# A 96-byte constant ahead of the left-hand SBUF pools of a hybrid decoder layer

## The chip, the cores and the metric

The kernel runs on one core of a Trainium2 chip. The metric is the device time of one launch in microseconds (us), as the median of several launches. The profile is one execution recorded by the hardware profiler; its engines are PE (TensorE matmul), PEld (TensorE weight load), DVE (VectorE), ACT (ScalarE), POOL (GpSimd) and SP (which issues the DMAs). SBUF is the on-chip memory from which PE reads both operands of a matmul: the weights (the stationary operand, 128x128 here, loaded ahead of the matmul) and the moving operand (up to 128x512 here). PSUM takes the products.

## The reference

One decoder layer on x of 1024 tokens by 1024 channels, in float32:

```python
h = rms_norm(x, norm1_g)
q, k, v, glu_a, glu_b = split(h @ w_in)            # 512 columns each
attn = stick_breaking_attention(rms_norm(q), rms_norm(k), v)   # 8 heads of 64, strictly causal
c = silu(layer_norm(causal_depthwise_conv(glu_a * sigmoid(glu_b))))   # width 31
x = x + concat([attn, c]) @ w_out
h = rms_norm(x, norm2_g)
gate, val = split(h @ w_up)                        # 2816 columns each
x = x + (silu(causal_depthwise_conv(gate)) * val) @ w_down    # width 3
```

## The kernel before, in words

Every large product is made in split precision: a float32 operand is split into a high part and a rest, both of type float32r, and three matmuls (high x high, high x rest, rest x high) are summed in one PSUM bank. The helper for it is `mm3`; the second argument of a matmul is the weights, the third is what moves past them.

```python
258     def mm3(ps, a_hi, a_lo, b_hi, b_lo, first, last):
259         nc.tensor.matmul(ps, a_hi, b_hi, start=first, stop=False)
260         nc.tensor.matmul(ps, a_hi, b_lo, start=False, stop=False)
261         nc.tensor.matmul(ps, a_lo, b_hi, start=False, stop=last)
```

In the profile a matmul is named `out<-moving,weights`, so `u<-b11h,a` has `b11h` moving past weights from `a`.

The layer runs in four stages. First come the input norm, the value, key and query projections and the GLU products with their convolution on DVE, ACT and POOL. Then comes the attention, whose instructions (with the last projections, the convolution's layer norm and its half of the output projection) are put in order by a planner in the kernel (`Plan`). The third stage finishes the output projection and the second norm and makes the up projection (`up`), 22 rounds over blocks of 128 hidden channels; it works in Strassen's manner, with seven products instead of eight, each of four `mm3`, so 84 matmuls of 128x512 in a round and 1848 in all. The fourth stage is the down projection (line 1203), 924 matmuls of 128x512 in the same manner.

SBUF is given out in pools. Pools without a side are stacked up from the low end ("left"), pools with `side="right"` are stacked down from the high end. The first left pool is `cst`, and each constant takes its place there in the order in which it is asked for. All other left pools (`small`, `mixp`, `qkvp`, `convp`, `op`, `wa`, `fp`) lie above it. In the built program each large tile of the left pools begins 128 bytes past a multiple of 256 in its partition, and each tile of the right pools that PE reads begins 224 bytes past one. The tiles that matter below are these:

```python
175     cst = ctx.enter_context(tc.tile_pool(name="cst", bufs=1))
281     hp = hp_ctx.enter_context(tc.tile_pool(name="hp", bufs=1, side="right", reuse_waits="tile"))
...
907     ffn = ffn_ctx.enter_context(tc.tile_pool(name="ffn", bufs=1, side="right", reuse_waits="tile"))
910         B[name] = [ffn.tile([P, 4, HS], F32R, tag=f"{name}{part}", name=f"b{name}{part}") for part in ("h", "l")]
...
996             pool, tag, bufs = {"11": (op, "v", 2) if f else (fp, "w", 8), "22": (op, "m", 1)}.get(name, (fp, "w", 8))
...
1052                 mm3(ps, ah[:, k, :], al[:, k, :], bh[:, k, :], bl[:, k, :], k == 0, k == 3)
...
1105         pool, bufs = (fp, 8) if n_slot % (8 + N_DN) < 8 else (dn, N_DN)
...
1203                         nc.tensor.matmul(ps, a[:, tok], b, start=first and m == 0, stop=last and m == 2,
```

- In the GLU products (`glu_b`, `glu_a`) the moving operand is the normed input (`h_hi`, `h_lo`, pool `hp`) and the weights come from pool `wp`: both are on the right.
- In the up projection (`u`, and `u_S` where a sum of blocks is used) the moving operand is `B` (pool `ffn`, right) and the weights are `A` (pools `fp` and `op`, left).
- In the down projection (`dn`) both operands of a matmul are named `wd`. They come from a ring of 28 slots: 8 in `fp` (left), then 20 in `dn` (right). Both operands of one matmul are on the same side; where the ring passes from one pool to the other, a matmul on one side alternates with the loading of weights on the other.

Operands for PE are made by ACT (the high part, L255 and L1114) and by DVE or POOL (the rest, L256 and L1115), and DVE (L1060 to L1067, L1206) brings the products out of PSUM.

Of the kernel before, what the change touches and what calls it, by code (L numbers as in the profile page):

```python
# [8 lines left out]
F32 = mybir.dt.float32  # L9
# [7 lines left out]
P = 128  # L17
# [120 lines left out]
def kernel(  # L138
# [60 lines left out]

    def const(shape, dt, name):  # L200
        return cst.tile(shape, dt, tag=name, name=name)

    ident = const([P, P], F32, "ident")
    make_identity(nc, ident)
    ident_b = const([P, P], BF16, "ident_b")
    nc.vector.tensor_copy(ident_b, ident)
    ident_r = const([P, P], F32R, "ident_r")
    nc.vector.tensor_copy(ident_r, ident)
    zero_b = const([P, P], BF16, "zero_b")
# [1033 lines left out]
```

## Time and profile before

| | |
|---|---|
| time, median of 3 runs | 1199.02 us (1198.83 to 1201.87) |
| the profiled execution's own time | 1199.73 us |
| its span, first to last instruction | 1197.9 us |
| mean granted TensorE clock | 0.985 |
| PE busy | 1146.3 us, 96% of the span |
| DVE, ACT, POOL busy | 954.4, 623.2, 611.1 us |

The span is 1.8 us shorter than the profiled execution's time, and that time is 0.7 us above the median of the runs. A matmul's duration in the profile is about 0.4 us, but matmuls overlap each other in the pipeline; what counts for the time is how far apart they start, and the view of the timeline shows their starts to a hundredth of a microsecond.

### The profile page before, as it was taken

The page shows a single profiled execution, that of the slowest core. Times are in us where ns is not written, and L with a number is a line of the kernel's source. Part 1 is how long each engine was busy: PE and PEld are TensorE (multiplying, and loading weights), DVE is VectorE, ACT ScalarE, POOL GpSimd, SP SyncE. Part 2 cuts the span into 40 slices and gives each one's busy share as a digit, 9 for nine tenths or more (in the row PEclk, how much of TensorE's full clock was granted, in tenths as well). Part 3 has the DMA queues.
Part 4 walks back from the last instruction along what each step waited for, and adds up shares of the span by engine and source line. Part 5 has one row for each costly group of instructions (what it writes and reads, how often), then busy time and mean ns, then how long its engine had stood idle before and what let it go on. Part 6 is the DMA issues. An engine that isn't in the chain of part 4 may idle for free.

```text
span 1197.9 us, 16127 instructions
## 1 busy us (share of the span) xinstructions
PE 1146.3 (96%) x5766; PEld 943.5 (79%) x5766; DVE 954.4 (80%) x1209; ACT 623.2 (52%) x1217; POOL 611.1 (51%) x490
## 2 busy tenths in 40 slices
PE   7999999999889798998999999999999999999998
PEld 6788999877668686776888888888888877888887
DVE  6699998777997987587977877787777578887877
ACT  6346674666666765364443333333333356666862
POOL 4347973555566753277523332233223157778873
PEclk9999999999999999998999999999999999999999
DMA  8122122111413222441322222222223261333033
GB/s 308 33 68 84 58 78 73 27 54 27 167 45 115 96 99 89 175 141 53 123 76 83 77 82 88 71 88 71 88 71 106 78 244 50 139 141 138 24 124 138
DMA packets 101853, 116.50 MB, mean 97 GB/s; under 512 B 20654, under 2 KB 80270, under 8 KB 101774
## 3 DMA queue, kind: packets, MB, share of 16 engines
q1 hardware_dynamic: 101486, 114.43, 28.6%
q8 instruction: 46, 0.75, 0.3%
q10 hardware_dynamic: 288, 1.05, 0.3%
q14 instruction: 33, 0.27, 0.1%
HBM read 82.95 MB, written 28.31 MB: 93 GB/s over the span
## 4 chain that ended last, share of the span: by engine, by line
PE 82%; DVE 7%; ACT 4%; POOL 3%; issue 2%; DMA 1%; SPq 0%; ACTq 0%; DVEq 0%; POOLq 0%
PE dn L1203 17%; PE u_S L261 7%; PE u_S L260 7%; PE u_S L259 7%; PE u L261 5%; PE u L260 5%; PE u L259 5%; PE wT L677 2%; DVE nb L651 2%; POOL conv_out L381 1%; PE v L261 1%; PE glu_b L259 1%; PE v L260 1%; PE v L259 1%; PE glu_b L260 1%
## 5 line engine op out<-in xcount | busy, mean ns | idle before, releaser
L1203 PE MATMUL dn<-wd,wd 128*128 128x512 f32 x924 | 216.0, 395 | 4.0 <-DVE c L1206 2.2
L1203 PEld LDWEIGHTS dn<-wd,wd 128*128 128x128 f32 x924 | 174.8, 190 | 45.1 <-DVE c L1206 3.7
L1206 DVE TENSOR_TENSOR c<-dn,c 128x512 f32<-128x512 f32 x144 | 95.3, 682 | 29.4 <-PE dn L1203 27.2
L375 DVE SCALAR_TENSOR_TENSOR conv<-cpad,cols_b,conv 128x1024 f32<-128x1024 f32 (+1 forms) x105 | 112.8, 1074 | 4.3 <-issue 1.5
L654 POOL TENSOR_TENSOR wt<-wt,nb 128x128 f32<-128x128 f32 (+3 forms) x64 | 77.4, 1212 | 75.6 <-DVE nb L651 51.9
L381 POOL TENSOR_TENSOR conv_out<-conv_out,attn_out 128x1024 f32<-128x1024 f32 (+1 forms) x40 | 83.0, 2074 | 52.4 <-ACT attn_out L380 49.8
L1114 ACT CAST wd<-rawd 128x512 fp32r<-128x512 f32 x154 | 85.4, 617 | 40.6 <-DMA rawd<-act_d 20.4
L1006 POOL TENSOR_TENSOR s<-rawu 128x512 f32<-128x512 f32 x21 | 31.2, 1487 | 136.2 <-DMA rawu<-in_w_up_dram 136.2
L651 DVE TENSOR_TENSOR_SCAN nb<-nb,one 128x128 f32<-128x128 f32 (+3 forms) x64 | 85.7, 1344 | 14.2 <-ACT nb L633 13.9
L255 ACT CAST aS<-rawu 128x512 fp32r<-128x512 f32 x66 | 41.0, 622 | 107.3 <-PE u_S L261 64.8
L1113 ACT COPY whole<-rawd 128x512 f32<-128x512 f32 x110 | 63.3, 585 | 41.2 <-DVE wd L1115 18.9
L1115 DVE TENSOR_TENSOR wd<-whole,wd 128x512 fp32r<-128x512 f32 x110 | 73.2, 681 | 5.4 <-ACT whole L1113 4.5
L1115 POOL TENSOR_TENSOR wd<-rawd,wd 128x512 fp32r<-128x512 f32 x44 | 57.3, 1326 | 34.6 <-ACT wd L1114 33.9
L255 ACT CAST a<-rawu 128x512 fp32r<-128x512 f32 x66 | 40.8, 621 | 60.0 <-PE u_S L261 38.2
L256 DVE TENSOR_TENSOR aS<-rawu,aS 128x512 fp32r<-128x512 f32 x66 | 71.0, 1077 | 1.2 <-ACT aS L255 0.6
L1070 DVE SCALAR_TENSOR_TENSOR y<-gv,cols_a,y 128x1023 f32<-128x1023 f32 (+1 forms) x44 | 61.4, 1396 | 12.3 <-ACT y L1068 12.3
L1012 POOL TENSOR_TENSOR rawu<-rawu 128x512 f32<-128x512 f32 x22 | 35.9, 1631 | 59.9 <-DVE a L256 57.8
L685 DVE TENSOR_TENSOR tl<-wT,rest 128x512 fp32r<-128x512 f32 x80 | 52.7, 678 | 14.3 <-ACT rest L681 14.0
L633 ACT ACTIVATE nb<-z 128x512 f32<-128x512 f32 (+2 forms) x96 | 47.8, 500 | 21.1 <-PE z L626 20.7
L256 DVE TENSOR_TENSOR a<-rawu,a 128x512 fp32r<-128x512 f32 x65 | 47.0, 724 | 14.6 <-ACT a L255 14.6
L677 PE MATMUL wT<-ident,wt 128*128 128x128 f32 x288 | 45.1, 279 | 11.0 <-DVE tl L685 3.5
L681 ACT CAST rest<-wT 128x512 fp32r<-128x512 f32 x57 | 33.0, 591 | 40.7 <-PE wT L677 32.0
(282 smaller groups left out, 3552.2 us busy)
## 6 DMA issues: line engine op xcount, KB each, us to landing
rawu<-in_w_up_dram SPq DMA_DIRECT2D x44, 512.0 KB, 4.0
act_d<-y SPq DMA_DIRECT2D x22, 512.0 KB, 2.6
rawd<-act_d SPq DMA_DIRECT2D x22, 512.0 KB, 3.3
rawd<-in_w_down_dram SPq DMA_DIRECT2D x22, 512.0 KB, 9.0
rawo<-in_w_out_dram SPq DMA_DIRECT2D x8, 512.0 KB
xt<-in_x_dram SPq DMA_DIRECT2D x8, 512.0 KB, 4.0
x_part<-xt SPq DMA_DIRECT2D x8, 512.0 KB, 2.6
x<-x_part SPq DMA_DIRECT2D x8, 512.0 KB
```

What stands on the lines that cost most here:

```text
L255: nc.scalar.copy(hi, src)
L256: lo_engine.tensor_tensor(lo, src, f32(hi), op=ALU.subtract)
L259: nc.tensor.matmul(ps, a_hi, b_hi, start=first, stop=False)
L260: nc.tensor.matmul(ps, a_hi, b_lo, start=False, stop=False)
L261: nc.tensor.matmul(ps, a_lo, b_hi, start=False, stop=last)
L375: nc.vector.scalar_tensor_tensor(own[:, a:b], src, tap(c, j), own[:, a:b], op0=ALU.mult, op1=ALU.add)
L381: nc.gpsimd.tensor_tensor(acc[:, a:b], acc[:, a:b], term, op=ALU.add)
L651: nc.vector.tensor_tensor_scan(rev, rev, one.to_broadcast([P, w]), 1.0, op0=ALU.mult, op1=ALU.bypass)
L1114: nc.scalar.copy(t[:, 0], src)
L1115: lo_engine.tensor_tensor(t[:, 1], whole, f32(t[:, 0]), op=ALU.subtract)
L1203: nc.tensor.matmul(ps, a[:, tok], b, start=first and m == 0, stop=last and m == 2, skip_group_check=True)
L1206: nc.vector.tensor_tensor(sums[c][s], ps, sums[c][s], op=ALU.add)
```

## The change

One constant of 24 float32 words, 96 bytes in each partition, is asked for before all others. Nothing writes or reads it.

```diff
     def const(shape, dt, name):
         return cst.tile(shape, dt, tag=name, name=name)
 
+
+    const([P, 24], F32, "pad")
+
     ident = const([P, P], F32, "ident")
     make_identity(nc, ident)
```

In the built program all five engines have the same instructions in the same order with the same waits as before; no instruction is added or moved. What differs are addresses: of the 905 tiles in SBUF, 462 begin 96 bytes higher (all those of the left pools), and 443 stay (the right pools and the fixed tiles at the bottom). The left tiles begin now 224 bytes past a multiple of 256, as the right ones do. Measured against multiples of 512, the left ones have gone from 128 to 224, and the right ones stand at 480. Lines of the changed kernel behind the constant have numbers higher by 3.

## The prediction

> **What bounds the kernel now.** I read the page first for the engines' shares, then the table by stretches of the span for the stage that the change could reach, then the waits in that stage, and at last the timeline, row by row, for the distance between matmuls. The change alters nothing but where the left tiles begin, so the one thing to look for is time that depends on where an operand lies.
>
> The page's head and the table by stretches (the columns are PE, PEld, DVE, ACT and POOL busy, then granted clock, DMA share and GB/s; 600 to 700 us lies in the up projection, 1000 to 1100 us in the down projection):
>
> ```profile
> PE 1146.3 (96%) x5766; PEld 943.5 (79%) x5766; DVE 954.4 (80%) x1209; ACT 623.2 (52%) x1217; POOL 611.1 (51%) x490
> 600.00:700.00 100.00, 100.00 (x431) 80.42 (x430) 74.77 (x87) 36.38 (x51) 28.11 (x20) 1.00 0.25 79
> 1000.00:1100.00 100.00, 100.00 (x439) 82.09 (x438) 85.60 (x141) 67.90 (x127) 81.16 (x64) 1.00 0.27 94
> ```
>
> PE never stands idle in these two stretches, at the full granted clock. Both are streams of 128x512 matmuls, and still 100 us hold 431 of them in the one and 439 in the other. A stream at the same clock that moves the same number of columns runs at two speeds.
>
> The waits between 600 and 960 us, longest first, have no row with PE on the left; the engines that prepare the up projection's operands wait for PE, not PE for them:
>
> ```profile
> ACT aS L255 <- PE u_S L261: 96.4, 44, 2.2
> ACT a L255 <- PE u_S L261: 36.1, 17, 2.1
> DVE gv L1064 <- PE u_S L261: 26.8, 18, 2.1
> ```
>
> So here a matmul that starts sooner shortens the span at once. The timeline (start in us, duration, engine, line, out<-moving,weights) gives the distance between starts. First the up projection, moving operand on the right (224 bytes past a multiple of 256), weights on the left (128 past one):
>
> ```profile
> 700.00 0.39 PE L260 MATMUL u<-b11l,a 128*128 128x512 f32 x1
> 700.23 0.40 PE L261 MATMUL u<-b11h,a 128*128 128x512 f32 x1
> 700.47 0.39 PE L259 MATMUL u<-b11h,a 128*128 128x512 f32 x1
> 700.70 0.39 PE L260 MATMUL u<-b11l,a 128*128 128x512 f32 x1
> ...
> 705.60 0.39 PE L260 MATMUL u_S<-bT2l,aS 128*128 128x512 f32 x1
> ```
>
> From the first row to the last there are 24 steps in 5.60 us: 233.3 ns each. Next the GLU products, both operands on the right:
>
> ```profile
> 115.18 0.39 PE L259 MATMUL glu_b<-h_hi,hi_glu_b 128*128 128x512 f32 x1
> ...
> 119.94 0.39 PE L259 MATMUL glu_a<-h_hi,hi_glu_a 128*128 128x512 f32 x1
> ```
>
> There are 21 steps in 4.76 us: 226.7 ns. The down projection has both kinds. Three stretches of it, each merged by the timeline into one row with its count; the ring of operand slots is on the right throughout in the first and the last, and passes between left and right in the middle one:
>
> ```profile
> 1074.83 15.35 PE L1203 MATMUL dn<-wd,wd 128*128 128x512 f32 x67
> 1094.81 17.47 PE L1203 MATMUL dn<-wd,wd 128*128 128x512 f32 x75
> 1112.81 15.58 PE L1203 MATMUL dn<-wd,wd 128*128 128x512 f32 x68
> ```
>
> Less one duration of 0.39 us, the first is 14.96 us for 66 steps, 226.7 ns; the last is 15.19 us for 67, 226.7 ns; the middle one is 17.08 us for 74, 230.8 ns. So the same line, between the same kinds of wait, goes slower just where a matmul on one side meets weights of the other.
>
> The groups by line show in which of the three matmuls of an `mm3` the excess sits (durations in ns at the row's end, before the idle time):
>
> ```profile
> L259 PE MATMUL u_S<-bT1h,aS 128*128 128x512 f32 x88 | 34.5, 392 | 0.0
> L260 PE MATMUL u_S<-bT1l,aS 128*128 128x512 f32 x88 | 34.7, 394 | 0.0
> L261 PE MATMUL u_S<-bT1h,aS 128*128 128x512 f32 x88 | 35.1, 398 | 0.0
> L260 PE MATMUL glu_a<-h_lo,hi_glu_a 128*128 128x512 f32 x64 | 24.9, 389 | 0.0
> ```
>
> A duration holds the step to the next matmul and a constant tail: 389 ns goes with a step of 226.7, so the tail is about 162 ns, and 392, 394 and 398 are steps of about 230, 232 and 236, on average 232.7, near the 233.3 of the timeline. In the timeline rows above the steps are the same for `b11` and up to `bT2`, although by the addresses of the built program the pairs of this stage are from 17 KB (`b21` with the last slot of `fp`) to 148 KB (`b22`) apart; and the operands of the GLU products, fast throughout, are up to 106 KB apart. So distance does not set the step. What the slow pairs have in common is the offset: 160 bytes from moving operand to weights, taken modulo 256 (96 where the sides are changed).
>
> **The change part by part.** Nothing runs for the constant: no engine writes or reads it, so its own cost is nothing, and the order of instructions and their waits is as before. What the move does is this.
>
> *The up projection.* Left tiles at 224 modulo 256 give both operands of `u` the same place of 256 bytes, as in the GLU products. I take the step of these: 233.3 - 226.7 = 6.6 ns less, for 22 x 84 = 1848 matmuls: 12.2 us. All of it is on the path, since the rows above have PE without a gap. What is late next is DVE: its 74.77 us in 100 become the same work in 97.2 us, 77%, and the waits above (ACT on PE, 96.4 us and 36.1 us) are the slack that is eaten first. The price of the new place has to be bounded from both sides, since the new offset is 0 modulo 256, but 256 modulo 512 (224 against 480), and no pair of this trace stands so: those on one side are all at 0 modulo 512. The nearest row is the same-side one, 226.7; the other end is the worst step seen with a mismatch, the 398 ns of L261, 236 ns a step, for all three matmuls. I take 226.7, because the pattern repeats in short lengths: from one block of k to the next the weights advance by 512 bytes and the moving operand by 2048, and the steps stay the same. So the pattern fits into 512 bytes a whole number of times. For a clean step at 256 its length must divide 256, and of the lengths that divide 512 only 512 itself does not.
>
> *The end of the up projection.* Behind it PE stands still for lack of sums and operands, and this has to move along with it, or part of the gain is lost. The chain that ended last, in time order:
>
> ```profile
> 974.33 0.25 PE dn L1203
> 974.75 5.04 DMA c<-x_d
> 979.89 0.64 DVE c L1206
> ```
>
> The load of `c` goes to the pool `dn`, which opens on the space of `B`; it is let go by the last matmul of `u`, so the stall of some 5 us follows `u` at the same distance. The gain passes through it whole. PE's granted clock is 0.83 between 980 and 1000 us by the table that follows, so the matmuls just behind the stall run slower; where this begins and ends can shift by a microsecond or two either way, and I put it in the range, not in the sum.
>
> ```profile
> 980.00:1000.00 20.00, 17.58 (x59) 12.47 (x60) 18.86 (x31) 8.23 (x17) 8.82 (x7) 0.83 0.61 226
> ```
>
> *The down projection.* The mixed stretch of 75 matmuls costs 230.8 - 226.7 = 4.1 ns each, 0.3 us; the ring turns five times so, 1.5 us. It goes if left and right pairs and those across all have one offset.
>
> *The attention and the rest.* There PE waits for others, and a faster matmul is partly lost in the next wait. The largest waits of PE in the whole span say how much is at stake:
>
> ```profile
> PE z L623 <- ACT wt L636: 5.3, 10, 0.9
> PE wT L677 <- DVE tl L685: 3.5, 4, 1.0
> ```
>
> In that stage `qk` and `op`, 384 matmuls of 128x512 with both operands on the right, come between transposes whose moving operand is on the left:
>
> ```profile
> L260 PE MATMUL qk<-lo_qk,h_hi 128*128 128x512 f32 x64 | 25.1, 392 | 0.0
> ```
>
> That is 3 ns above the 389 of GLU; for 384 it makes 1.2 us at most. I count 0.4.
>
> *DVE, ACT, POOL.* They read and write the left tiles at a new place. Two rows of the same form, one with its SBUF operands on the left (gv) and one on the right (tl):
>
> ```profile
> L1206 DVE TENSOR_TENSOR gv<-dn,gv 128x512 f32<-128x512 f32 x48 | 31.7, 679 | 0.5 <-PE dn L1203 0.5
> L685 DVE TENSOR_TENSOR tl<-wT,rest 128x512 fp32r<-128x512 f32 x80 | 52.7, 678 | 14.3 <-ACT rest L681 14.0
> ```
>
> 679 ns at 128 and 678 ns at 224 modulo 256: nothing either way.
>
> The sum is 12.2 + 1.5 + 0.4 = 14.1 us. From the profiled execution's 1199.73 us that leaves 1185.6; the median of the runs is 0.7 lower, and 1199.0 - 14.1 = 1184.9, which I round to 1185.0.
>
> [...]
>
> **The rivals.**
>
> *No change* (1199.0). The slow steps come from something else that mixed pairs share, for instance that two far parts of SBUF are read at once, and the offset is a bystander. For it: in this trace mixed side and mixed offset are never apart. Against it: the equal steps over pairs of tiles near and far. The sum is then 0, and the time 1199.0. [...]
>
> *In part* (1191 to 1195). An offset of 256 modulo 512 is better than the old one but not clean, as the mixed stretch of `dn` is, at 230.8. Then u gives (233.3 - 230.8) x 1848 = 4.6 us and little else: 1194.4; at 229 it is 7.9 us: 1191. Chance 0.08.
>
> *Slower* (1204). The two reads meet in every matmul when they are half of 512 bytes apart, and all three of an `mm3` take the step of the worst now, 236 ns. Then u costs (236 - 233.3) x 1848 = 5.0 us more: 1204.0. It decides where u's step stands above 233.3. For it: L261 shows that such a step exists, and no pair here has this offset. Against it: of the lengths that divide 512, only 512 itself would bring it about. Chance 0.08.
>
> *The change doesn't do what it says.* The constant is never used and could have been dropped from the pool. The built program excludes this: 462 tiles begin 96 bytes higher.
>
> **How the numbers follow.** The forecast has 0.75: 1185.0, by itself from 1181 (all of 1.2 us in the attention, 0.5 more around the ring, 2 us of clock behind the stall) to 1189 (some of the steps stay at 228). The range of 8 in 10 reaches over it and over the case in part: 1181 to 1194.5. About 0.3%, 3.6 us, is what a measurement of this kernel can tell from no change. Forecast and part lie below 1195.4: faster 0.83; same 0.09; slower 0.08.
>
> **What would show it.** Right: in the timeline of the changed kernel the steps of u are 226 to 227 ns and the three lines L259 to L261 (higher by 3 there) have one duration of about 389; 100 us of the up projection hold some 443 matmuls; the mixed stretches of dn come down to 226.7; the load of `c` still follows the last `u` by less than 1 us; DVE, ACT and POOL keep their means. Wrong: u at 233 again (then side, not offset), or at 236 (the rival on the slower side), or u at 227 and the time back in a longer stall before `dn` or in waits of PE for DVE in the up projection.

## The result, and the profile after

The changed kernel takes 1186.54 us (median of 4 runs, 1185.87 to 1188.44) beside 1199.32 us for the kernel before; the ratio is 0.9892, 95% interval 0.9873 to 0.9911. That is 1.1% less. The profiled execution takes 1185.9 us, with a span of 1184.1, against 1199.73 and 1197.9: 13.8 us less.

The table by stretches, 600 to 700 us (up projection; PE, PEld, DVE, ACT and POOL busy, clock, DMA share, GB/s), has 442 matmuls in 100 us where there were 431:

```profile
600.00:700.00 100.00, 100.00 (x442) 82.78 (x442) 74.62 (x91) 37.91 (x55) 26.89 (x19) 1.00 0.27 85
```

The timeline of the same stage gives the step; its lines are those of `mm3`, higher by 3:

```profile
700.00 0.39 PE L264 MATMUL u<-b21h,a 128*128 128x512 f32 x1
700.23 0.39 PE L262 MATMUL u_S<-bT2h,aS 128*128 128x512 f32 x1
700.46 0.39 PE L263 MATMUL u_S<-bT2l,aS 128*128 128x512 f32 x1
...
705.90 0.39 PE L263 MATMUL u_S<-bT1l,aS 128*128 128x512 f32 x1
```

From the first to the last there are 26 steps in 5.90 us: 226.9 ns, where it was 233.3. In the groups by line, the three matmuls of an `mm3` have become alike (392, 394 and 398 ns before), while `qk`, whose operands were always on one side, stays where it was:

```profile
L264 PE MATMUL u_S<-bT1h,aS 128*128 128x512 f32 x88 | 34.2, 389 | 0.0
L262 PE MATMUL u_S<-bT1h,aS 128*128 128x512 f32 x88 | 34.2, 389 | 0.0
L263 PE MATMUL u_S<-bT1l,aS 128*128 128x512 f32 x88 | 34.2, 389 | 0.0
L263 PE MATMUL qk<-lo_qk,h_hi 128*128 128x512 f32 x64 | 25.1, 392 | 0.0
```

A mixed stretch of `dn`, in the timeline:

```profile
1081.66 17.61 PE L1206 MATMUL dn<-wd,wd 128*128 128x512 f32 x77
```

Less 0.39 us it is 17.22 us for 76 steps, 226.6 ns; the same stretch stood at 230.8.

Where the 13.8 us come from can be read from the first and last start of two groups. First the kernel before (duration least, median, most; first and last start), then the changed one:

```profile
L259 PE MATMUL u<-b11h,a x88: 392/392/628, 533.2 to 956.7; 128*128 128x512 f32 x88
L1203 PE MATMUL dn<-wd,wd x924: 387/389/796, 974.2 to 1193.8; 128*128 128x512 f32 x185
```

```profile
L262 PE MATMUL u<-b11h,a x88: 389/389/628, 532.6 to 944.4; 128*128 128x512 f32 x88
L1206 PE MATMUL dn<-wd,wd x924: 387/389/504, 961.4 to 1180.0; 128*128 128x512 f32 x185
```

The up projection starts 0.6 us earlier. From its start to that of `dn` it was 441.0 us and is 428.8, 12.2 less. From the first matmul of `dn` to its last it was 219.6 and is 218.6, 1.0 less. The sum is 13.8.

### The profile page after: what moved, and what is told of

Its sections match the earlier page's. It is cut to its first block, busy times and chain, and to the rows that moved or that the text cites. A ratio compares the mean times of both kernels' runs of the same rounds, so it can differ in the third digit from the quotient of the medians.

```text
span 1184.1 us, 16127 instructions
## 1 busy us (share of the span) xinstructions
PE 1129.5 (95%) x5766; PEld 940.1 (79%) x5766; DVE 942.4 (80%) x1209; ACT 623.0 (53%) x1217; POOL 610.0 (52%) x490
## 4 chain that ended last, share of the span: by engine, by line
PE 72%; DVE 10%; ACT 7%; POOL 5%; DMA 4%; issue 3%; SPq 0%; ACTq 0%; DVEq 0%; POOLq 0%
PE dn L1206 10%; PE u_S L262 7%; PE u_S L264 7%; PE u_S L263 7%; PE u L264 5%; PE u L262 5%; PE u L263 5%; PE wT L680 2%; ACT wd L1117 2%; DVE nb L654 2%; DMA rawd<-act_d 2%; DVE conv L378 1%; POOL conv_out L384 1%; PE glu_b L262 1%; PE glu_b L263 1%
## 5 line engine op out<-in xcount | busy, mean ns | idle before, releaser
L1206 PE MATMUL dn<-wd,wd 128*128 128x512 f32 x924 | 212.8, 391 | 6.2 <-DVE c L1209 3.7
L1073 DVE SCALAR_TENSOR_TENSOR y<-gv,cols_a,y 128x1023 f32<-128x1023 f32 (+1 forms) x44 | 58.3, 1325 | 10.8 <-ACT y L1071 10.8
L259 DVE TENSOR_TENSOR aS<-rawu,aS 128x512 fp32r<-128x512 f32 x66 | 62.6, 951 | 1.9 <-ACT aS L258 1.6
L1015 POOL TENSOR_TENSOR rawu<-rawu 128x512 f32<-128x512 f32 x22 | 33.5, 1524 | 57.2 <-DVE a L259 55.1
L1011 POOL TENSOR_TENSOR rawu<-s,rawu 128x512 f32<-128x512 f32 x21 | 31.2, 1489 | 50.4 <-DVE a L259 49.6
```

The costliest lines, as they stand in the source:

```text
L259: lo_engine.tensor_tensor(lo, src, f32(hi), op=ALU.subtract)
```

## The experiments

Each kernel stands on the one before or on the changed one, as its diff says. "Offset" is the place of the weights less that of the moving operand, in bytes, modulo 256; it was 160 in the up projection before the change and is 0 after. Operands at offset 0 are called in step, all others out of step. Steps for which no timeline is shown are means over at least 35 starts of a profiled execution, and each of the three maps is one execution. The diffs are excerpts, and the remarks behind `#` are added here.

**A map of offsets, all else taken away.** A kernel with nothing but matmuls; block after block, one operand is moved by 4 words.

```diff
+    for o in range(0, 132, 4):
+        series(0, o)      # weights moved
+    for o in range(0, 132, 4):
+        series(o, 0)      # moving operand moved
```

> A kernel of its own that computes nothing of the layer: 68 blocks of 48 matmuls of 128x512 in the order of the up projection (high x high, high x rest, rest x high), back to back, with nothing else running. In the first 33 measured blocks the weights are moved by 16 bytes from block to block, from 0 to 512 bytes past the place of the moving operand; in the next 33 the moving operand is moved so and the weights stay. Theory (offset, period 256): step 226 to 228 ns at offsets of 0, 256 and 512 bytes, 232 to 234 at 96 and 160 from the moving operand to the weights (236 at the worst of the three), and the two halves of 512 alike. Rival (a shorter period): clean at 128 as well, or at 64, 128, 192. Rival (side): 226 to 228 everywhere, since all tiles lie on one side.

Two blocks in the timeline, the first in step, the second 96 bytes out of step:

```profile
22.88 0.39 PE L95 MATMUL b<-move,weights 128*128 128x512 f32 x1
...
33.53 0.39 PE L97 MATMUL b<-move,weights 128*128 128x512 f32 x1
```

```profile
100.24 0.39 PE L95 MATMUL b<-move,weights 128*128 128x512 f32 x1
...
110.78 0.40 PE L95 MATMUL b<-move,weights 128*128 128x512 f32 x1
```

47 steps in 10.65 us are 226.6 ns, and 45 in 10.54 us are 234.2 ns. All blocks, ns per step:

| offset | 0 | 16 | 32 | 48 | 64 | 80 | 96 | 112 | 128 | 144 | 160 | 176 | 192 | 208 | 224 | 240 |
|---|---|---|---|---|---|---|---|---|---|---|---|---|---|---|---|---|
| weights moved | 226.7 | 226.9 | 233.2 | 233.2 | 233.2 | 231.9 | 234.2 | 233.2 | 233.4 | 233.4 | 233.3 | 229.8 | 229.0 | 233.2 | 233.3 | 226.7 |
| moving operand moved | 226.7 | 226.7 | 233.3 | 234.7 | 233.3 | 233.3 | 234.4 | 233.3 | 232.3 | 231.1 | 233.3 | 231.1 | 228.9 | 233.3 | 233.3 | 231.6 |

The second half of 512 bytes repeats the first within 0.1 ns in each series. So the period is 256, not 128 or 64 and not 512; the loss needs neither two sides of SBUF nor another engine; and 160, the offset of the kernel before, gives the 233.3 ns that the kernel before had. The two series differ from each other by up to 4.9 ns (at 240), so away from 0 the offset is not all that sets the step.

**The same side, out of step.** The kernel before with 96 bytes between two right pools:

```diff
+    gap = in_ctx.enter_context(tc.tile_pool(name="gap", bufs=1, side="right"))
+    gap.tile([P, 24], F32, tag="gap", name="gap")
     wp = in_ctx.enter_context(tc.tile_pool(name="wp", bufs=2, side="right", reuse_waits="tile"))
```

> The kernel before, with 96 unused bytes between the right pools hp (normed input) and wp (weights), so that two operands on the same side are 96 bytes out of step in the GLU products and the projections. Theory (offset): the step of GLU goes from 226.7 to about 233 ns, the up projection stays at 233; 384 GLU matmuls cost 2.5 us, the 192 of qk 1 us, the projections of 256 columns an unknown little: the time is 1202 to 1206. Rival (side): GLU stays at 226.7 and the time at 1199.

The timeline of the GLU products:

```profile
115.22 0.39 PE L259 MATMUL glu_b<-h_hi,hi_glu_b 128*128 128x512 f32 x1
...
119.88 0.40 PE L261 MATMUL glu_a<-h_hi,lo_glu_a 128*128 128x512 f32 x1
```

20 steps in 4.66 us are 233.0 ns, from 226.7. The time is 1202.27 us, ratio 1.0018 (1.0007 to 1.0029), at the lower end of what was expected. The side is not what counts; the rival of "no change" rested on it and falls. The projections of 256 columns go the other way, which takes part of the loss back: their median steps are 117 to 119 ns, from 120.

**The pad at the other end.** The kernel before, its right tiles moved and its left ones not:

```diff
+    edge = ctx.enter_context(tc.tile_pool(name="edge", bufs=1, side="right"))
+    edge.tile([P, 24], F32, tag="edge", name="edge")
```

> The kernel before, with the 96 unused bytes at the top of the right pools instead of at the bottom of the left ones: the right tiles begin 128 bytes past a multiple of 256, where the left ones begin, and the left ones stay. Theory (it is the offset between the two operands that counts): as the changed kernel, u and dn at 226.7 ns, the time 1186 to 1188. Rival (it is the place of the left tiles that was bad, 128 past a multiple of 256): u stays at 233 or worse, the time at 1199 or above.

The time is 1186.69 us, ratio 0.9885 (0.9868 to 0.9902), the same gain; 600 to 700 us holds 443 matmuls.

**Both pads.** The changed kernel with the same two lines.

> The changed kernel with the 96 unused bytes at the top of the right pools as well: left tiles at 224, right tiles at 128 past a multiple of 256, each side where the other was. Theory (offset): the gain is gone, u at 232 to 234 ns, since the offset is 96 instead of 160 modulo 256; the time 1197 to 1200. Rival (the place of the left tiles): the gain stays, 1186.

The time is 1201.98 us, ratio 1.0012 (1.0002 to 1.0023): the gain is gone and a little more, where 1197 to 1200 was expected. The table by stretches (PE, clock, DMA share, GB/s) of the one-pad kernel above and of this one:

```profile
600.00:700.00 100.00, 100.00 (x443) 1.00 0.27 85
```

```profile
600.00:700.00 100.00, 100.00 (x428) 1.00 0.25 79
```

428 matmuls is less than the 431 of the kernel before, and fits the map: the steps of u average 234.3 ns, and the offset is 96 here, which has 234.2 to 234.4 ns there, against 233.3 at 160. These two runs settle that it is the place of one operand against the other that counts, not that of the left tiles.

**Other lengths of the pad.** In the changed kernel:

```diff
-    const([P, 24], F32, "pad")
+    const([P, 8], F32, "pad")      # 32 bytes; the other: [P, 88], 352 bytes
```

> The changed kernel with a constant of 32 bytes instead of 96: left tiles at 160, right at 224 past a multiple of 256, so in the up projection the weights are 192 bytes past the moving operand. By the first map a step of 229.0 ns at 192: (233.3 - 229.0) x 1848 = 7.9 us off the time before, 1191 to 1192. If only the exact place counts and everything else is alike: 1199.

> The changed kernel with a constant of 352 bytes: left and right tiles at the same place of 512 bytes too (480). Theory (period 256): as with 96 bytes, u at 226.7 ns, 1186 to 1188. Rival (512 matters as well): u below 226.7 and the time under 1184.

With 32 bytes the time is 1192.9 us, ratio 0.9937 (0.9919 to 0.9955), and the steps of u average 228.9 ns; the map had 229.0 at that offset, which made 1191 to 1192 of it, 1 us too little. With 352 bytes, where both sides stand at the same place of 512 as well, it is 1189.07 us, ratio 0.9908 (0.9888 to 0.9928), 1 us above what was expected, with u at 226.7 ns: not below the changed kernel, so 512 adds nothing.

**Whose weights, how finely, and 256 columns.** A second map.

```diff
+    for o in range(0, 68, 4):
+        series(0, o, 256)
+    for o in range(1, 9):
+        series(0, o)
+    crossed([(0, 0), (0, 0)])       # (place of moving operand, place of weights), in words
+    crossed([(0, 0), (24, 24)])
+    crossed([(0, 24), (24, 0)])
+    ...
```

> A kernel of its own that computes nothing of the layer, blocks of 48 matmuls as in the first map. First 17 blocks of 256 columns, the weights 0 to 256 bytes past the moving operand in steps of 16: the up-to-now reading of the gap run (projections of 256 columns went from 120 to 117 to 119 ns out of step) says 120 ns in step and 117 to 120 elsewhere; a rival says 120 plus up to 7 ns as for 512 columns. Then 512 columns with the weights 4 to 32 bytes past in steps of 4: clean to 16 and slow from 32 by the first map; the edge tells whether it is a line of 16 or of 32 bytes. Last, pairs of matmuls in turn, 96 bytes apart. Theory A (a matmul's moving read meets the load of the NEXT weights): the pair (0,0),(96,96) is slow, about 233, though each matmul is in step with its own weights, and the pair (0,96),(96,0) is clean, 227, though each is out of step with its own. Theory B (own weights): the reverse.

With 256 columns the step is 120.0 ns in step, 113.3 at offsets of 64 and 192, and 116.6 to 120.0 at the others. In the table by stretches (offset 0, then 64):

```profile
34.00:39.00 5.00, 5.00 (x44) 1.00 0.00 0
57.00:62.00 5.00, 5.00 (x47) 1.00 0.01 3
```

With 512 columns, 4 bytes out of step already cost: 232.4 ns, and 229.8 to 235.0 up to 32 bytes. At 16 bytes this map has 233.4, coming there from a block at 229.8, and the first, with the operands at the same places, 226.9, coming from a block in step. So what went before can decide the step near 0; but a slow block before does not always make the next one slow: in the second series of the first map, the block at 16 bytes has 226.7 and comes behind the one at 32, which has 233.3. At 0 every block of 512 columns in the three maps ends at 226.7.

The pairs, in bytes: (0,0),(0,0) 226.7 ns; (0,0),(96,96) 233.9; (0,96),(96,0) 229.8, in turn 224 and 236; (0,96),(0,96) 234.3. With 160 instead of 96 the second and the third have 234.1 and 230.2. In the traces of the maps the load of the next weights starts 2 to 4 ns behind a matmul of 128x512 and takes about 188 ns, less than the 224 to 236 ns from one start to the next. A matmul that is in step with its own weights is slow when the next weights are out of step, as theory A says; that the reverse pair stands half way, where A had 227, it does not explain. So the place of the next weights counts, and not it alone.

**Does the order count?** Blocks in eight orders, in step and 96 bytes out of step.

```diff
+        [(m, i % 8) for i, m in enumerate(moves * 2)],    # new weights each time
+        [(m, 0) for m in moves],                          # one set of weights
+        [(m, 0) for m in one],                            # one set, one moving block
+        ...
```

> A kernel of its own that computes nothing of the layer: blocks of 60 matmuls of 128x512, all tiles in step modulo 256 in the first half, weights 96 bytes past in the second. Between the blocks stands one in the order of the kernel (high x high, high x rest, rest x high), in which two of three matmuls load new weights. The second map had in-step blocks in another order, with new weights for each matmul and the moving tiles in turn, at 233.9 ns. Theory (the order counts as well as the place): in step, the kernel's order stands at 226.7 each time, the orders with new weights for each matmul at 233 to 234, those that repeat the weights at 226.7. Rival (something in the moving operand's order): the block with one set of weights and many moving blocks is slow too. Rival (what came before decides): the order of the kernel is slow after a slow block. Out of step by 96: the kernel's order at 234, and a block with one set of weights and one moving block shows whether a load of the same weights collides at all.

The expectation rests on a misreading of the second map: its block at 233.9 ns was the pair (0,0),(96,96), and the one in step had 226.7. With that put right there was nothing left for the order to explain, and the run shows the same. Stretches of the first half and of the second:

```profile
120.00:260.00 140.00, 140.00 (x620) 1.00 0.00 0
275.00:505.00 230.00, 230.00 (x983) 1.00 0.00 1
```

Every order has 226.7 ns in step and 234.2 to 234.4 out of step, even where the same weights are loaded again and the same block moves past them. The first block shows one thing more: after the 427 ns of its start its steps are 233, 236, 224, 231, 236, 228, 233, 231 and then 227. A stream in step needs several matmuls to find its pace: eight here, and five to nine at the like places of the other two maps.

**A version that should be faster still.** The changed kernel, with the projections' weights (256 columns, the moving operand there) begun 64 bytes further in longer slots; beside it the changed kernel itself once more, and two variants.

```diff
+        if shape == [4, 256]:
+            hi, lo = [pool.tile([P, D + 64], F32R, tag=hi_tag, name=f"{part}_{name}", bufs=bufs)[:, 16:16 + D].rearrange(
+                "p (k n) -> p k n", n=256) for part in ("hi", "lo")]
```

> The changed kernel, with the weights of the value, key and query projections begun 64 bytes further in their slots (the slots 256 bytes longer). Their matmuls have 256 columns, and the second map shows 113.3 ns for these at offsets of 64 and 192 against 120.0 in step. Theory: 768 matmuls go from 120.0 to 113.3 ns, 5.1 us in stages where PE has few gaps: 1181 to 1183. Rival (these stages wait for ACT and POOL, which make the squares and the roots of the keys and queries): under 1 us, 1186.

> The changed kernel as it is, beside the version with the shifted projection weights: 1186 to 1188, as before.

> The changed kernel, with the weights of the value, key and query projections begun 192 bytes further in their slots instead of 64. In these projections they are the moving operand, so the stationary one is now 64 bytes past it (modulo 256) instead of 192. With 64, the version before stood at 117.7 ns a step, not at the 113.3 of the second map. If the map's other clean place holds where the map's own places (multiples of 64) are not kept: 113.3 ns, 768 x 6.7 = 5.1 us, 1181 to 1183. If it takes places at multiples of 64, as all rows of the map have: again about 118 ns and 1186.

> The kernel before with its right tiles at 128 past a multiple of 256 (so both sides stand at 128, a multiple of 64) and the projections' moving weights 64 bytes further, at 192, so that the stationary operand is 192 past it: the same two places modulo 64 as in the second map, whose step at 192 was 113.3 ns. If the place modulo 64 counts beside the offset: 113.3 ns and 1181 to 1183. If it does not: about 118 ns as in the version before, 1186.

The first was expected at 1181 to 1183 us. The times are 1186.46 us (ratio 0.9884, 0.9868 to 0.9899), 1187.9 for the changed kernel beside it (0.9895, 0.9877 to 0.9913), 1185.06 with 192 bytes (0.9883, 0.9865 to 0.9902) and 1186.82 with both sides at 128 (0.9889, 0.9870 to 0.9908). The groups of the query projection, in the changed kernel and in the two versions with 64 and 192 bytes:

```profile
L263 PE MATMUL q<-lo_q,h_hi 128*128 128x256 f32 x64 | 18.1, 283 | 0.0
```

```profile
L263 PE MATMUL q<-lo_q,h_hi 128*128 128x256 f32 x64 | 17.9, 279 | 0.0
```

```profile
L263 PE MATMUL q<-lo_q,h_hi 128*128 128x256 f32 x64 | 17.7, 277 | 0.0
```

With 64 bytes the step is about 118 ns instead of 113.3, and so it mostly is with both sides at 128, so that the place modulo 64 is not the reason. With 192 bytes, q runs at 113 and k mostly at 118, in one execution and at one offset: in this form the stream can settle at either pace, and what chooses is open. By the mean steps there (115.0, 116.7 and 113.4 ns for v, k and q, from 120) the three projections take some 3.8 us less, but all four intervals overlap, and none of these versions is shown to beat the changed kernel.

## Why the prediction was right

*The up projection* was put at 12.2 us, 6.6 ns for each of 1848 matmuls; it measured 12.2. The choice in that step, to take 226.7 ns for an offset that the trace did not show (0 modulo 256, 256 modulo 512), is what the first map bears out: it repeats after 256 bytes. The argument for it was weaker than the prediction puts it. From one block of k to the next the place of one operand against the other moves by 2048 - 512 = 1536 bytes, so equal steps there, taken alone, leave lengths of 384 and 768 open beside those that divide 512. And no row of that trace spoke against a length of 512 itself; that it is one length among many is no measure of its chance. So it was worked out that the offset counts, and the length of 256 was in part luck.

In the first map, where the other engines stand still, the step depends on the place of the weights against the moving operand: 226.7 ns in step and 234.2 with the weights 96 bytes further, 7.5 ns more.

*The end of the up projection* follows `u` as was said: the loads of `c` begin 0.8 us behind its last matmul, as before. But the chain there is another one; the load of `c` took 5.04 us before and was followed by work of DVE, and now a second load stands behind it:

```profile
964.21 5.68 DMA c<-x_d
969.95 7.92 DMA rawd<-in_w_down_dram
```

The second profile of the same kernel has that second load too, with 7.71 us at 969.35. The kernels with the pad at the other end and with 352 bytes, which have the same step, have the chain of before, `c` followed by DVE. So the faster step alone does not bring it, and what does is open.

*The down projection* was put at 1.5 us. Its mixed stretches are clean, and the steps under 260 ns of the whole stage sum to 1.5 us less (900 of them to 206.0 us before, 901 to 204.5 after); the stage is 1.0 us shorter, since its longer steps sum to 0.5 us more in this execution. In the second profile of the same kernel the longer steps sum to 12.4 us instead of 14.1, so they vary by more than this from one execution to the next. The uncertainty was foreseen in the range, but put down to the clock. The clock cost less here: before, it was 0.83 between 980 and 1000 us, with ten steps of 427 ns, and now it is 1.00 in the whole stage. The longer waits stand where the chain above has its loads.

*The attention* was put at 0.4 us, and that term was wrong: `qk` stays at 392 ns, and the steps of `qk` and `op` together come to 0.1 us less. Their offset was 0 before. They stand above 389 because they come in short runs between transposes: of the 33 runs of `qk`, 19 have three matmuls and the longest has 15, and in the changed kernel the second to the sixth step of a run are 231 to 233 ns in the median, and those from the seventh on 227 to 228. That is the settling of the map of orders. The 0.6 us by which the up projection starts sooner is not from there by these rows, and is no more than runs of one kernel differ by.

*DVE* keeps its 679 and 678 ns, as foreseen. The sum was 14.1 us; the profiled executions differ by 13.8 and the medians by 12.8, with runs of one kernel 2.6 us apart.

The rivals: "no change" fell with the gap on one side (GLU from 226.7 to 233.0) and the pad at the other end (0.9885). "In part" is what 32 bytes give: u at 228.9 ns and 1192.9 us, in the range that was worked out for it. "Slower" is what both pads give, by an offset of 96 rather than by 256.

## What to carry to other kernels

When PE streams matmuls without gaps, read the step between their starts, not the duration, and compare stages whose matmuls have one shape: a difference of 3% (here 233.3 against 226.7 ns) may be in where the operands lie. In these runs two operands of 128x512 float32r matmuls did best at the same place of 256 bytes in the partition (226.7 ns, against 228.9 to 234.7 at 32 to 224 bytes); a constant of a few bytes ahead of a pool does it, here at the cost of 96 bytes in each partition and of no time. For 256 columns that was not the best place (120.0 ns there, 113.3 at 64 and 192 bytes), so measure each shape.

## What the runs showed of the hardware

- A back-to-back float32r matmul of 128x512 takes 226.7 ns from start to start with its weights at offset 0 modulo 256, and 228.9 to 234.7 at 32 to 224; one of 128x256 takes 120.0 at offset 0 and 113.3, half of 226.7, at 64 and 192.
- The excess repeats after 256 bytes (the two halves of 512 alike within 0.1 ns), on one side of SBUF and with no other engine at work. Four bytes out of step are enough for it (232.4 ns).
- After a disturbance, a stream in step takes five to nine matmuls (233, 236, 224, 231, 236, 228, 233, 231 in one case) to come back to 227 ns; one 96 bytes out of step does not in the 60 matmuls of a block.
- The load of the next weights starts 2 to 4 ns behind a matmul of 128x512 and takes about 188 ns, so it is over before the next matmul starts, 224 to 236 ns after the one before.
- Near a clean place and with 256 columns, a stream can settle at one of two paces (226.9 or 233.4 at 16 bytes; 113 or 118 for 256 columns at 64). What chooses was not found, and neither was the reason for the length of 256.
